# First feed-forward layer of a decoder trunk: six plain pairs instead of seven, operand sums made earlier and in tiles of their own

## The chip, the cores and the metric

The kernel runs on one core of one Trainium2 chip. The metric is the device time of one launch in microseconds (us). Before the change the median of three runs is 2024.97 us (2024.91 to 2026.1).

## The reference

The computation is a decoder trunk of two layers for one sequence of 512 positions and 1024 channels, all in float32. Each layer is a half-weight feed-forward, a mixer (a gated recurrence beside windowed attention) and a second half-weight feed-forward. Only the first feed-forward of layer 0 is touched:

```python
def swiglu(h, w_gate, w_up, w_down):
    return (jax.nn.silu(h @ w_gate) * (h @ w_up)) @ w_down
...
        h = rms_norm(x, gn[0])
        x = x + 0.5 * rms_norm(swiglu(h, w_ffn1_gate[l], w_ffn1_up[l], w_ffn1_down[l]), gn[1])
```

`w_gate` and `w_up` are 1024 x 2816, so there are 22 blocks of 128 hidden channels. For each, a gate product and an up product of 128 x 1024 by 1024 x 512 are needed: one *pair*.

## The kernel before

The activations lie with the channels on the partitions: eight tiles of 128 channels x 512 positions. Every float32 operand is cut into a high part in a reduced format and the low rest, and a product is made of three matrix products, high by high, high by low and low by high (`mm3`, line 412). All products pass through `mm`, so nearly every matmul has line 116.

A pair is made in one of two ways. The *plain* way (`project`, twice) takes 2 x 8 channel tiles x 3 products of 512 columns. The *seven-product* way (`sevenths`) treats the pair as 2 x 2 blocks (gate or up; upper or lower channels; early or late positions) and makes seven block products of 256 columns instead of eight, 7 x 4 x 3 in all. For that it needs sums and differences of the activation tiles: `sums()` makes them for one channel tile k and its partner k+4. Four calls serve all pairs of the layer.

In the first feed-forward of layer 0 the norm is not known when the first products start. So the plain pairs run on x times the gain, and their outputs are scaled afterwards by `rb`, the inverse root mean square spread over the partitions (`gated`, lines 1098 to 1104). `sums()` of the class `First` starts from scaled rows instead: x times gain times `rb` (line 566), then three high/low splits of half tiles (lines 432 and 433: a cast on ScalarE, a subtraction on VectorE), four half-tile sums (lines 490 to 497), and two more splits of 512 columns. That is two scalings, nine further VectorE instructions and five ScalarE casts per call.

Meanwhile x itself is turned to position-major tiles and written to memory (`lay`): eight groups of four 128 x 128 transposes (line 126), each group into one bank of the pool `aux`, copied out by ScalarE and VectorE in turn (line 555) and written by SyncE (line 556). The pool `aux` has three banks; the pool `acc`, for projections, five.

The order of TensorE's instructions is the order in which the code issues them; side jobs such as `lay` are coroutines that are let in when a counter of estimated TensorE time passes their due time (`order.poll`). On the other engines a scheduler orders the instructions by priority. Each engine then works its list strictly in order and waits on counters of the others. Weights come in through SyncE's queue into four buffers, are split by ScalarE (`whi`, line 359) and by VectorE or an adding transfer of GpSimd (`wlo`, lines 363 and 358) into six buffers each.

`FIRST = 7` is the number of plain pairs of this layer; the other 15 are seven-product pairs. `fast(pre, a, FIRST)` makes those.

Of the kernel before, what the change touches and what calls it, by code (L numbers as in the profile page):

```python
# [11 lines left out]
ALU = mybir.AluOpType  # L12
# [21 lines left out]
    head=2600.0, level=5000.0, last=3400.0, chunks=2600.0, states=2600.0, norm=2370.0, gate=8000.0,  # L34
    values=1200.0, scores=2000.0, exp=9000.0, shares=6000.0, turn=1900.0, turned=3000.0, rest=1200.0, lent=4200.0, apart=4000.0, block=2000.0, pair=4000.0, att0=1260.0, att1=12300.0,
)
W32, WS, AHEAD, TAIL, FIRST, EARLY, LATE = 4, 6, 3, 4, 7, 4, 8
TURN = 0
SEVEN = 16
ASIDE = 16  # L40
# [6 lines left out]
def trunk(ctx: ExitStack, tc: tile.TileContext, xin, wall, gains, lbT, hgain, sinks, c_dist, c_mask, c_ident, out):  # L47
    nc = tc.nc
# [11 lines left out]
    def nm(s):  # L60
        seq[0] += 1
        return f"{s}_{seq[0]}"

    def big(dt=F32, shape=None):
        return sb.tile(shape or [P, S], dt, tag="s", name=nm("s"), bufs=SLOTS)
# [10 lines left out]
    def const(shape, name, dt=F32):  # L76
        return cp.tile(shape, dt, tag=name, name=name)
# [35 lines left out]
    order = Order()  # L113
# [16 lines left out]
    g_sb = const([P, DEPTH, 6, KT], "g_sb")  # L130
    nc.scalar.dma_start(g_sb, gains)
    xs = [big() for _ in range(KT)]
# [26 lines left out]
    class Stream:  # L159
# [98 lines left out]
        def quarter(self, it):  # L258
# [16 lines left out]
            if it.kind in ("p1", "p2"):  # L275
                w = raw((u if it.kind == "p1" else v) + q)
            elif it.kind in ("p3", "p5"):
                w = self.b22[q]
            elif it.kind == "p7":

                w = self.b12[q]
                if q == 0:
                    sums(w, w, self.b22[q], ALU.add)
            else:
                w = self.b12[q]
# [5 lines left out]
            if it.kind == "p7" and q + 1 < it.n:  # L291
                sums(self.b12[q + 1], self.b12[q + 1], self.b22[q + 1], ALU.add)
            elif it.kind == "p6":
                sums(self.b22[q], self.b22[q], w, ALU.add)
# [191 lines left out]
    def quarter_sums(a11, a12, a21, a22, flip=False):  # L486


        s, t = big(F32, [P, 2, S // 2]), big(F32, [P, 2, S // 2])
        nc.vector.tensor_tensor(s[:, 0, :], a22, a21, op=ALU.subtract)  # L490
        nc.vector.scalar_tensor_tensor(s[:, 1, :], s[:, 0, :], -1.0, a11, op0=ALU.mult, op1=ALU.subtract)
        if flip:
            nc.vector.tensor_tensor(t[:, 0, :], s[:, 1, :], a12, op=ALU.add)
            nc.vector.tensor_tensor(t[:, 1, :], a21, a11, op=ALU.subtract)
        else:
            nc.vector.scalar_tensor_tensor(t[:, 0, :], s[:, 1, :], -1.0, a12, op0=ALU.mult, op1=ALU.subtract)
            nc.vector.tensor_tensor(t[:, 1, :], a11, a21, op=ALU.subtract)
        return s, t

    def pair_split(v, how=split):  # L500
        return how(v, to=(big(F32R, [P, 2, S // 2]), big(F32R, [P, 2, S // 2])))
# [13 lines left out]
    class First(Quarters):  # L515
# [44 lines left out]
        def sums(self):  # L560

            k = len(self.x56)
            a = []
            for i in range(2):
                f = xs[k + 4 * i]
                nc.vector.scalar_tensor_tensor(f, f, g_sb[:, 0, 0, k + 4 * i : k + 4 * i + 1], self.rb, op0=ALU.mult, op1=ALU.mult)
                a.append([f[:, c] for c in HALF])
            self.x124.append([])
            for v in (a[0][0], a[1][0], a[1][1]):
                x = big(F32R, [P, 2, S // 2])  # L570
                split(v, to=(x[:, 0, :], x[:, 1, :]))
                self.x124[k].append(x)
            for x, v in zip((self.x56, self.x37), quarter_sums(a[0][0], a[1][0], a[0][1], a[1][1])):
                x.append(pair_split(v))
# [420 lines left out]
    def quad(pre, halves):  # L995

        o = [acc() for _ in range(4)]
        blocks = {}
        ws.pinned = halves
        for half in (0, 1) if halves else (None,):  # L1000
            c = WHOLE if half is None else HALF[half]
            for k in range(KT):
                order.until(lambda: pre.have[half or 0] > k)
                for j in range(4):
                    if (k, j) not in blocks:
                        blocks[k, j] = ws.next(uses=2 if halves else 1)
                    if halves and (k, j) == (0, 2):
                        lead(o[j][:, c], blocks[k, j][2], pre.h[k][0][:, c], LEAD_IN[half])
                    wmm(o[j][:, c], blocks[k, j], cut(pre.h[k], c), k == 0, k == KT - 1)
            ws.pinned = False  # L1010
        return o

    def project(pre, get=acc):
        o = get()
        for k in range(KT):
            wmm(o, ws.next(), pre.h[k], k == 0, k == KT - 1)
        return o
# [55 lines left out]
    def fast(pre, a, start):  # L1073
        def early():
            if j == FT - 1:
                for i in range(SEVEN, SEVEN + EARLY):
                    ws.part[i] = split(a[i])

        ws.tight = True
        for j in range(start, FT):  # L1080
            ws.most = AHEAD + (j < FT - 1)
            m = sevenths(pre, early, j == start)
            z = big(F32, [P, 2, H2])
            ws.hold(nc.scalar.activation(out=m[:, 0:2, :], in_=m[:, 0:2, :], func=AF.Silu))

            def gate(m=m, z=z):
                ws.hold(nc.vector.scalar_tensor_tensor(z, m[:, 0:2, :], -1.0, m[:, 2:4, :], op0=ALU.mult, op1=ALU.mult))

            ws.gate = gate
            if j == FT - 1:  # L1090
                ws.product()
            a.append(z.rearrange("p i t -> p (i t)"))
        ws.tight = False

    def ffn(l, n, pre, nxt, halves=True):
        a = []

        def gated(og, ou):
            z, u = big(), big()
            if first:  # L1100
                pin(nc.vector.tensor_tensor(z, og, pre.rb, op=ALU.mult))
                nc.scalar.activation(out=z, in_=z, func=AF.Silu)
                nc.vector.tensor_tensor(u, ou, pre.rb, op=ALU.mult)
                nc.vector.tensor_tensor(u, u, z, op=ALU.mult)
            else:
                nc.scalar.activation(out=z, in_=og, func=AF.Silu)
                pin(nc.vector.tensor_tensor(u, ou, z, op=ALU.mult))
            a.append(u)

        first = isinstance(pre, First)  # L1110
        o = quad(pre, halves)
        if first:
            o.append(project(pre))
            o.append(project(pre, aux))
            order.until(lambda: pre.rb is not None)
        if not first:
            pre.sums()
            pre.sums()
        for j in range(2):
            gated(o[2 * j], o[2 * j + 1])  # L1120
        if first:
            gated(o[4], o[5])
            for j in range(3, FIRST):
                if j > 3:
                    order.until(lambda: pre.laid)
                    pre.sums()
                if j == 4:
                    pre.sums()
                if j == FIRST - 1:
                    ws.most = AHEAD + 2  # L1130
                gated(project(pre), project(pre))
            fast(pre, a, FIRST)
        else:
            pre.sums()
            ws.most = AHEAD + 2
            og = project(pre)
            pre.sums()
            gated(og, project(pre))
            fast(pre, a, 3)
        return down(a, FT, l, n + 1, nxt, True)  # L1140
# [357 lines left out]
    pre = First()  # L1498
# [68 lines left out]
    for l in range(DEPTH):  # L1567
        pre = ffn(l, 0, pre, (l, 2), halves=l > 0)
        pre = mixer(l, pre, (l, 4))
        pre = ffn(l, 4, pre, (l + 1, 0) if l + 1 < DEPTH else None)  # L1570
# [81 lines left out]
```

## Time and profile before

| What | Value |
|---|---|
| Median of three runs | 2024.97 us |
| The profiled execution | 2024.79 us, span 2023.0 us |
| TensorE busy | 2016.2 us, 100% |
| VectorE busy | 1624.3 us, 80% |
| ScalarE busy | 1265.2 us, 63% |
| Granted TensorE clock | 1.0 in all slices |

A busy TensorE means that matmuls follow each other; their ends are modelled, and the next one starts before the last one ends. So the cost of a matmul is read from the distance between starts. The same holds for VectorE and ScalarE, where a row's time reaches a little past the start of the next row. Times at the left of a row are from the start of the span.

### The profile page before, as it was taken

The page shows a single profiled execution, that of the slowest core. Times are in us where ns is not written, and L with a number is a line of the kernel's source. Part 1 is how long each engine was busy: PE and PEld are TensorE (multiplying, and loading weights), DVE is VectorE, ACT ScalarE, POOL GpSimd, SP SyncE. Part 2 cuts the span into 40 slices and gives each one's busy share as a digit, 9 for nine tenths or more (in the row PEclk, how much of TensorE's full clock was granted, in tenths as well). Part 3 has the DMA queues.
Part 4 walks back from the last instruction along what each step waited for, and adds up shares of the span by engine and source line. Part 5 has one row for each costly group of instructions (what it writes and reads, how often), then busy time and mean ns, then how long its engine had stood idle before and what let it go on. Part 6 is the DMA issues. An engine that isn't in the chain of part 4 may idle for free.

```text
span 2023.0 us, 36425 instructions
## 1 busy us (share of the span) xinstructions
PE 2016.2 (100%) x13553; PEld 1809.1 (89%) x13553; DVE 1624.3 (80%) x2894; ACT 1265.2 (63%) x2213; POOL 268.3 (13%) x318
## 2 busy tenths in 40 slices
PE   9999999999999999999999999999999999999998
PEld 8899988877898999998899998898778989999987
DVE  5888899767786788888998888977686858888888
ACT  7566687447364566658766666864554646666684
POOL 0111140000000011113211111400000100111140
PEclk9999999999999999999999999999999999999999
DMA  8688798311246368879768888872122554788794
GB/s 257 159 193 198 177 203 244 109 63 64 83 104 208 112 158 190 193 189 208 202 170 196 196 190 203 189 223 86 61 74 63 151 182 123 170 193 200 175 202 122
DMA packets 166801, 328.07 MB, mean 162 GB/s; under 512 B 19072, under 2 KB 85088, under 8 KB 166624
## 3 DMA queue, kind: packets, MB, share of 16 engines
q1 hardware_dynamic: 122416, 228.16, 34.1%
q0 software_dynamic: 44064, 97.54, 28.5%
q8 instruction: 106, 1.74, 0.3%
q14 instruction: 71, 0.58, 0.1%
q10 hardware_dynamic: 144, 0.05, 0.0%
HBM read 213.43 MB, written 14.73 MB: 113 GB/s over the span
## 4 chain that ended last, share of the span: by engine, by line
PE 93%; DVE 3%; ACT 1%; DMA 1%; issue 1%; SPq 0%; DVEq 0%; ACTq 0%
PE acc L116 71%; PE aux L116 20%; PE aux L126 2%; DVE wlo L296 1%; DVE s L264 1%; DMA w<-wall 1%; PE acc L126 0%; ACT whi L288 0%; DVE s L968 0%; SPq L244 0%; ACT s L442 0%; ACT s L443 0%; DVE wlo L363 0%; DVE s L863 0%; DVE s L433 0%
## 5 line engine op out<-in xcount | busy, mean ns | idle before, releaser
L116 PE MATMUL acc<-s,whi 128*128 128x256 f32 (+1 forms) x4998 | 1018.9, 303 | 0.0
L116 PEld LDWEIGHTS acc<-s,whi 128*128 128x128 f32 x4998 | 791.5, 188 | 46.6 <-issue 3.2
L116 PE MATMUL acc<-s,wlo 128*128 128x256 f32 (+1 forms) x2488 | 752.5, 302 | 0.1
L116 PEld LDWEIGHTS acc<-s,wlo 128*128 128x128 f32 x2488 | 467.9, 188 | 23.3 <-DVE wlo L363 0.4
L116 PE MATMUL acc<-whi,s 128*128 128x512 f32 x1360 | 441.5, 393 | 0.0
L359 ACT CAST whi<-w 128x1024 fp32r<-128x1024 f32 (+1 forms) x310 | 286.1, 926 | 195.0 <-PE acc L116 124.5
L358 POOL DMA_DIRECT2D wlo<-w x178 | 154.6, 869 | 1200.2 <-ACT wlo L355 715.0
L116 PEld LDWEIGHTS acc<-whi,s 128*128 128x128 f32 x1360 | 255.3, 188 | 57.1 <-issue 3.2
L116 PE MATMUL acc<-wlo,s 128*128 128x512 f32 x680 | 265.5, 390 | 0.2 <-DVE wlo L296 0.2
L355 ACT ACTIVATE wlo<-w 128x1024 fp32r<-128x1024 f32 (+1 forms) x178 | 154.6, 869 | 137.1 <-PE aux L116 98.2
L116 PE MATMUL aux<-s,whi 128*128 128x256 f32 (+1 forms) x1296 | 226.9, 278 | 0.0
L359 ACT CAST whi<-tt 128x1024 fp32r<-128x1024 f32 x160 | 168.4, 1053 | 83.2 <-DVE tt L341 43.0
L363 DVE TENSOR_TENSOR wlo<-w,whi 128x1024 fp32r<-128x1024 f32 (+1 forms) x132 | 157.4, 1205 | 78.3 <-ACT whi L359 78.1
L363 DVE TENSOR_TENSOR wlo<-tt,whi 128x1024 fp32r<-128x1024 f32 x160 | 195.4, 1221 | 9.9 <-ACT whi L359 7.3
L116 PEld LDWEIGHTS aux<-s,whi 128*128 128x128 f32 x1296 | 195.8, 188 | 1.1 <-issue 0.5
L116 PE MATMUL aux<-s,wlo 128*128 128x256 f32 (+1 forms) x648 | 179.8, 277 | 0.0
L116 PEld LDWEIGHTS acc<-wlo,s 128*128 128x128 f32 x680 | 127.8, 188 | 27.0 <-DVE wlo L296 2.1
L116 PE MATMUL aux<-whi,s 128*128 128x512 f32 x432 | 143.7, 390 | 0.0
L444 POOL DMA_DIRECT2D s<-s x128 | 111.1, 967 | 223.5 <-ACT s L432 104.7
L116 PEld LDWEIGHTS aux<-s,wlo 128*128 128x128 f32 x648 | 121.6, 188 | 0.4
L296 DVE TENSOR_TENSOR wlo<-s,whi 128x512 fp32r<-128x512 f32 x160 | 102.7, 686 | 9.9 <-ACT whi L288 9.9
L1070 DVE TENSOR_TENSOR m<-aux,s 128x512 f32<-128x512 f32 x80 | 55.2, 690 | 52.0 <-PE aux L116 51.5
(184 smaller groups left out, 2485.1 us busy)
## 6 DMA issues: line engine op xcount, KB each, us to landing
w<-wall SPq DMA_DIRECT2D x267, 512.0 KB, 3.9
wlo<-w POOLq DMA_DIRECT2D x98, 512.0 KB, 5.4
w<-wall SPq DMA_DIRECT2D x224, 128.0 KB, 3.5
wlo<-w POOLq DMA_DIRECT2D x80, 256.0 KB, 4.2
s<-wall SPq DMA_DIRECT2D x128, 128.0 KB, 4.2
s<-s POOLq DMA_DIRECT2D x64, 256.0 KB, 4.6
x_d<-s SPq DMA_DIRECT2D x48, 256.0 KB, 4.7
s<-x_d SPq DMA_DIRECT2D x48, 256.0 KB, 5.1
```

The costliest lines, as they stand in the source:

```text
L116: nc.tensor.matmul(o, lhsT, rhs, start=start, stop=stop)
L126: nc.tensor.transpose(o, src, ident)
L264: pin(nc.vector.tensor_tensor(o[c], x[c], y[c], op=op))
L296: pin(nc.vector.tensor_tensor(it.lo[:, h[c]], w[c], it.hi[:, h[c]].bitcast(F32), op=ALU.subtract))
L355: i = nc.scalar.mul(it.lo[:, c], w[:, c], -1.0)
L358: nc.gpsimd.dma_start(it.lo[:, c].bitcast(F32), w[:, c], accum_op=ALU.add)
L359: i = nc.scalar.copy(it.hi[:, c], w[:, c])
L363: self.hold(nc.vector.tensor_tensor(it.lo[:, c], w[:, c], it.hi[:, c].bitcast(F32), op=ALU.subtract))
L444: nc.gpsimd.dma_start(lo.bitcast(F32), src, accum_op=ALU.add)
L1070: ws.hold(nc.vector.tensor_tensor(m[:, 1:3, :], pairs[2], v[:, ::-1, :], op=ALU.add))
```

## The change

`FIRST` goes from 7 to 6. The scaled rows of `sums()` are written to new tiles, no longer over x; so `sums()` needs not wait until `lay` has read x, and the condition on `pre.laid` is gone. The four calls now stand ahead of the fourth, fifth and sixth plain pair (one, one and two); before, two stood ahead of the fifth and one each ahead of the sixth and seventh.

```diff
-W32, WS, AHEAD, TAIL, FIRST, EARLY, LATE = 4, 6, 3, 4, 7, 4, 8
+W32, WS, AHEAD, TAIL, FIRST, EARLY, LATE = 4, 6, 3, 4, 6, 4, 8
...
             for i in range(2):
-                f = xs[k + 4 * i]
-                nc.vector.scalar_tensor_tensor(f, f, g_sb[:, 0, 0, k + 4 * i : k + 4 * i + 1], self.rb, op0=ALU.mult, op1=ALU.mult)
+                f = big()
+                nc.vector.scalar_tensor_tensor(f, xs[k + 4 * i], g_sb[:, 0, 0, k + 4 * i : k + 4 * i + 1], self.rb, op0=ALU.mult, op1=ALU.mult)
                 a.append([f[:, c] for c in HALF])
...
             for j in range(3, FIRST):
-                if j > 3:
-                    order.until(lambda: pre.laid)
+                pre.sums()
+                if j == FIRST - 1:
                     pre.sums()
-                if j == 4:
-                    pre.sums()
-                if j == FIRST - 1:
                     ws.most = AHEAD + 2
                 gated(project(pre), project(pre))
             fast(pre, a, FIRST)
```

The change moves instructions on ScalarE and VectorE. In the rows below a name is a tile with its running number, and the brackets name the counters waited for. First TensorE in the fourth plain pair, at the fourth group of transposes, which goes to `aux_520` before and to `aux_547` in the change. Before:

```order
L116 MATMUL acc_513<-s_132,whi_338 128x512 [waits DVE_49]
L116 MATMUL acc_513<-s_133,whi_338 128x512
L116 MATMUL acc_513<-s_132,wlo_339 128x512
L116 MATMUL acc_513<-s_144,whi_338 128x512
L116 MATMUL acc_513<-s_145,whi_338 128x512
L116 MATMUL acc_513<-s_144,wlo_339 128x512
L126 MATMUL aux_520<-ident,s_74 128x128 [waits DVE_49]
```

In the change:

```order
L116 MATMUL acc_540<-s_132,whi_338 128x512
L116 MATMUL acc_540<-s_133,whi_338 128x512
L116 MATMUL acc_540<-s_132,wlo_339 128x512
L116 MATMUL acc_540<-s_144,whi_338 128x512
L116 MATMUL acc_540<-s_145,whi_338 128x512
L116 MATMUL acc_540<-s_144,wlo_339 128x512
L126 MATMUL aux_547<-ident,s_74 128x128 [waits PE_49,Activation_49]
```

The place on TensorE is the same; the counter waited for is now ScalarE's. The value waited for is that of the copy that empties the bank of the first group of transposes, `s_502<-aux_497`. Before, it was VectorE's line 1103, which empties the bank of the third pair's up projection.

Next ScalarE, from the second pair's SiLU (`s_445`) and the third's (`s_451`) to the copies of line 555. Before:

```order
L1102 ACTIVATE s_445<-s_445 128x512 [waits DVE_49]
L555 COPY s_475<-aux_470 128x512 [waits PE_49]
L1102 ACTIVATE s_451<-s_451 128x512 [waits DVE_49]
L359 CAST whi_671<-w_72_384 128x1024 [waits DMAHW7_49,PE_49,Activation_49]
L555 COPY s_510<-aux_505 128x512 [waits PE_49]
L355 ACTIVATE wlo_672<-w_72_384 128x1024
L555 COPY s_539<-aux_534 128x512 [waits PE_49]
```

In the change:

```order
L1102 ACTIVATE s_445<-s_445 128x512 [waits DVE_49]
L1102 ACTIVATE s_451<-s_451 128x512 [waits DVE_49]
L432 CAST s_461<-s_457 128x256 [waits DVE_49]
L359 CAST whi_675<-w_72_384 128x1024 [waits DMAHW7_49,PE_49,Activation_49]
L432 CAST s_464<-s_459 128x256 [waits DVE_49]
L432 CAST s_467<-s_459 128x256
L355 ACTIVATE wlo_676<-w_72_384 128x1024 [waits PE_49]
L432 CAST s_476<-s_470 128x512 [waits DVE_49]
L432 CAST s_480<-s_471 128x512 [waits DVE_49]
L555 COPY s_502<-aux_497 128x512
L555 COPY s_537<-aux_532 128x512 [waits PE_49]
```

The copy of the first group (`s_475<-aux_470` before, `s_502<-aux_497` now) stood one place behind a SiLU; it now stands behind five casts of the first `sums()` and two instructions of a weight split.

Last VectorE, at the end of the fourth `sums()`, in the change. Ahead of it stand all the other three calls, the fourth and fifth pair's scaling of outputs and the weight sums of the first two seven-product pairs:

```order
L566 SCALAR_TENSOR_TENSOR s_748<-s_73,g_sb,s_395 128x512 [waits DMAHW1_49]
L566 SCALAR_TENSOR_TENSOR s_750<-s_77,g_sb,s_395 128x512
L433 TENSOR_TENSOR s_752<-s_748,s_752 128x256 [waits Activation_49]
L345 TENSOR_TENSOR tt_848<-tt_845,w_104_530 128x512
L363 TENSOR_TENSOR wlo_844<-tt_845,whi_843 128x1024 [waits DMASW3_49,PE_49,Activation_49]
L433 TENSOR_TENSOR s_755<-s_750,s_755 128x256 [waits Activation_49]
L433 TENSOR_TENSOR s_758<-s_750,s_758 128x256 [waits Activation_49]
L490 TENSOR_TENSOR s_761<-s_750,s_748 128x256
L497 TENSOR_TENSOR s_762<-s_748 128x256
L491 SCALAR_TENSOR_TENSOR s_761<-s_761,s_748 128x256 [waits DVE_49]
L496 SCALAR_TENSOR_TENSOR s_762<-s_761,s_750 128x256 [waits DVE_49]
L433 TENSOR_TENSOR s_768<-s_761,s_767 128x512 [waits DMAHW3_49,Activation_49]
```

Before, the scalings of this call stood far ahead, among the first two calls, and the weight sums of the second seven-product pair began only behind line 496. From the second seven-product pair on, the lists of all engines are the same in both kernels but for the tiles' numbers, and so is everything behind the layer. On SyncE the eight writes of line 556 now stand together, behind the weight loads of the first two seven-product pairs; before, two loads stood among them. The row of `rows_d` stands ahead of the eighth write now, and behind it before.

## The prediction

> **What bounds the kernel now.** I read the page's first part and its chain first, then the busy times by stage, then the engines' instructions in order of time between 40 and 108 us. From the page:
>
> ```profile
> PE 2016.2 (100%) x13553; PEld 1809.1 (89%) x13553; DVE 1624.3 (80%) x2894; ACT 1265.2 (63%) x2213; POOL 268.3 (13%) x318
> ...
> PE 93%; DVE 3%; ACT 1%; DMA 1%; issue 1%; SPq 0%; DVEq 0%; ACTq 0%
> ```
>
> TensorE hardly pauses, and 93% of the chain that ended last is its own work. So a matmul removed is time won, and any pause that appears on TensorE is time lost: nothing behind it has slack to take it up. The busy times by stage around the change:
>
> ```profile
> core 0: us, PE busy (x) PEld busy (x) DVE busy (x) ACT busy (x) POOL busy (x), PEclk, DMA share, GB/s
> ...
> 40.00:60.00 20.00, 20.00 (x106) 16.68 (x105) 11.52 (x20) 11.47 (x18) 2.58 (x3) 1.00 0.93 235
> 60.00:80.00 20.00, 20.00 (x90) 16.58 (x89) 19.66 (x40) 10.65 (x19) 0.86 (x1) 1.00 0.56 142
> 80.00:100.00 20.00, 20.00 (x142) 18.56 (x141) 16.42 (x28) 11.53 (x18) 3.44 (x4) 1.00 0.53 128
> 100.00:120.00 20.00, 20.00 (x178) 20.00 (x178) 16.70 (x25) 13.16 (x17) 3.44 (x4) 1.00 0.85 195
> ```
>
> TensorE never waits in these stages. VectorE is full between 60 and 80 us, where the four `sums()` run, and has 8.5 us free in the twenty before. The change moves `sums()` into that free stretch, and takes one plain pair's time away from them.
>
> **The plain pair: -1.36 us.** TensorE's rows of a plain pair, of the start of the seven-product pairs, and the chain through two of the latter:
>
> ```profile
> 82.83 0.62 PE L116 MATMUL acc<-s,whi 128*128 128x512 f32 x2
> ...
> 88.27 0.51 PE L116 MATMUL acc<-s,whi 128*128 128x144 f32 x3
> ...
> 98.07 6.80 PE acc L116 x60
> 104.87 2.72 PE aux L116 x24
> 107.59 6.80 PE acc L116 x60
> ```
>
> From 82.83 to 88.27 lie the last eight channel tiles, 24 products of 512 columns: 5.44 us, 0.2267 each. A plain pair has 48: 10.88. A seven-product pair repeats after 107.59 - 98.07 = 9.52 us (84 products of 256 columns). The difference is 1.36. The lead product of 144 columns is made once in both kernels. The number of `sums()` is the same, and one more seven-product combination on VectorE and ScalarE lies beside TensorE work there, as in the other 15 pairs.
>
> **The fourth group of transposes: +2.5 us.** `aux` has three banks. The fourth group needs the bank of the first; the copy that frees it now stands on ScalarE behind five casts of the first `sums()` and a weight split, and two of the casts wait for VectorE. The rows for this, TensorE, ScalarE and VectorE one after the other:
>
> ```profile
> 49.12 0.60 PE L126 MATMUL aux<-ident,s 128*128 128x128 f32 x4
> 52.80 0.60 PE L126 MATMUL aux<-ident,s 128*128 128x128 f32 x4
> ...
> 44.28 0.59 ACT L555 COPY s<-aux 128x512 f32<-128x512 f32 x1 [0.64 <-PE aux L126]
> ...
> 47.31 1.05 ACT L359 CAST whi<-w 128x1024 fp32r<-128x1024 f32 x1 [1.67 <-PE acc L116]
> 48.27 0.58 ACT L555 COPY s<-aux 128x512 f32<-128x512 f32 x1
> 48.74 1.06 ACT L355 ACTIVATE wlo<-w 128x1024 fp32r<-128x1024 f32 x1
> ...
> 56.08 1.06 ACT L355 ACTIVATE wlo<-w 128x1024 fp32r<-128x1024 f32 x1
> 57.04 0.62 ACT L1102 ACTIVATE s<-s 128x512 f32<-128x512 f32 x1
> ...
> 62.04 0.62 ACT L432 CAST s<-s 128x512 fp32r<-128x512 f32 x1
> 62.56 1.05 ACT L355 ACTIVATE wlo<-w 128x1024 fp32r<-128x1024 f32 x1
> ...
> 80.61 0.70 ACT L432 CAST s<-s 128x256 fp32r<-128x256 f32 x2
> ...
> 44.89 0.68 DVE L1103 TENSOR_TENSOR s<-aux,s 128x512 f32<-128x512 f32 x1
> ...
> 59.67 0.42 DVE L490 TENSOR_TENSOR s<-s,s 128x256 f32<-128x256 f32 x1
> 60.01 0.42 DVE L497 TENSOR_TENSOR s<-s 128x256 f32<-128x256 f32 x1
> ```
>
> The first copy ran at 44.28, long before 49.12. In the change ScalarE goes on thus. The cast of `whi` starts at 47.31 as before, since it waits for the first plain projection of this pair to let go of its buffer. Start to start, a 1024-column instruction takes 0.96 (56.08 to 57.04, 47.31 to 48.27), a cast of 512 takes 0.52 (62.04 to 62.56), a cast of 256 takes 0.30 (two in 0.70, the last 0.40). So the casts of `s_464` and `s_467` start at 48.27 and 48.57, the `wlo` at 48.87, the cast of `s_476` at 49.83. The cast of `s_480` waits for VectorE: `s_464` is there at 48.68, then two subtractions, line 491 and line 497 at 0.34 each (59.67 to 60.01), and line 496 with its full 0.42, which ends at 50.46. With 0.04 for each handing over, the cast starts at 50.5, the copy at 51.0, and ends 0.59 later at 51.6. TensorE stands at the transposes from 49.12 to 51.65: 2.5 us, with all its later work behind it. From below, ScalarE's list alone without VectorE's wait gives 47.31 + 0.96 + 0.60 + 0.96 + 0.52 + 0.52 + 0.59 = 51.46, so 2.3; from above, each of the six instructions ahead of the copy with its full time, 0.1 more, gives 3.1. The later copies follow at once and empty the other banks: group five comes 1.8 us behind, no further wait.
>
> **The operands of the first seven-product pair: +1.5 us.** VectorE's copy of the sixth group follows its transposes, so 2.5 us later than in this row:
>
> ```profile
> 53.44 0.69 DVE L555 COPY s<-aux 128x512 f32<-128x512 f32 x1 [2.98 <-PE aux L126]
> ...
> 63.60 0.75 DVE L566 SCALAR_TENSOR_TENSOR s<-s,g_sb,s 128x512 f32<-128x512 f32 x1
> 64.27 1.70 DVE L433 TENSOR_TENSOR s<-s,s 128x512 fp32r<-128x512 f32 x4
> ...
> 74.38 1.29 DVE L433 TENSOR_TENSOR s<-s,s 128x512 fp32r<-128x512 f32 x2 [0.27 <-ACT s L432]
> ...
> 76.19 0.69 DVE L341 TENSOR_TENSOR tt<-w 128x512 f32<-128x512 f32 x1
> 76.79 0.69 DVE L343 TENSOR_TENSOR tt<-tt,w 128x512 f32<-128x512 f32 x1
> ...
> 78.12 1.22 DVE L363 TENSOR_TENSOR wlo<-tt,whi 128x1024 fp32r<-128x1024 f32 x1
> 79.26 0.68 DVE L1101 TENSOR_TENSOR s<-acc,s 128x512 f32<-128x512 f32 x1
> ...
> 85.14 0.69 DVE L433 TENSOR_TENSOR s<-s,s 128x512 fp32r<-128x512 f32 x1
> ```
>
> At about 56.55 the fourth pair's line 1101 starts. From there to `s_768`, the split of the fourth call's differences, VectorE's list has 19 instructions of 512 columns at 0.60 (76.19 to 76.79), six scalings at 0.66 (63.60 to 64.27), 21 of 256 at 0.335 and three of 1024 at 1.14 (78.12 to 79.26): 11.4 + 4.0 + 7.0 + 3.4 = 25.8. I add 2.3 of waits, an estimate put together from the same rows: 0.4 for the fourth pair's SiLU, which stands behind a late copy; 0.4 for the end of the fifth pair's up projection; 0.6 for a cast of the third call behind a weight split on ScalarE; 0.4 for the last cast of the chain; 0.5 in small steps. So `s_768` is there at 56.55 + 25.8 + 2.3 + 0.69 = 85.3. TensorE begins the seven-product pairs at 88.27 - 10.88 + 2.5 = 79.9 and wants `s_768` as the fourth channel tile of the third product, after 34 products of 0.1133 and the lead: 83.8. It waits 1.5. As a cross-check: before, the same split ended at 85.8 and was wanted at 92.2, 6.4 to spare; the wish moves up 8.4, the split 0.5. From below, without the waits, it comes at 83.0 and nothing is lost: 0. From above, with twice the waits, 3.8. I take 1.5. The next operand, 0.6 later, is wanted 1.4 later.
>
> **Costed at nothing.** The weights: transfers of the third seven-product pair stand on SyncE behind the eight writes of line 556. Counted along VectorE's list from 56.55, the last copy ahead of them falls at about 64, and the first weight sums, which free their buffers, end at about 67; they are wanted at about 92. GpSimd's adding transfers start in the same relation to their products. The tiles for scaled rows free themselves within the call. If that cover were gone, each late weight would stop TensorE directly.
>
> **The sum**: -1.36 + 2.5 + 1.5 = +2.6 us. The profiled execution took 2024.79 us (span 2023.0 and 1.8 around it), 0.2 below the median of the runs: 2027.4 against the one, 2027.6 against the other. I say 2027.5, 0.13% above before.
>
> **Rivals.** About 0.2%, or 4 us, is what a measurement of this kernel can tell from no change.
>
> *No pause appears* (10%). ScalarE's copy comes in time and VectorE keeps up, so the pair's 1.36 us are won: 2024.97 - 1.36 = 2023.6. For it: VectorE's 8.5 free us between 40 and 60. Against it: the list on ScalarE has no way past the `wlo` and the casts, and the 49.12 - 47.31 = 1.8 us hold only three of the six instructions ahead of the copy.
>
> *TensorE falls back to its starting speed after the pause* (8%), slower than before. The start of the kernel and a product of the same kind later:
>
> ```profile
> 1.07 4.96 PE L116 MATMUL aux<-ones 128*128 128x128 f32 x24 [1.07 <-DVE eps_t L139]
> ...
> 35.94 1.02 PE L116 MATMUL aux<-s,ones 128*128 128x512 f32 x2
> 36.39 1.02 PE L116 MATMUL aux<-s,whi 128*128 128x512 f32 x2
> 37.25 0.40 PE L116 MATMUL aux<-s,wlo 128*128 128x512 f32 x1
> ```
>
> Twelve float32 products of 128 columns (two records each) took 4.96 us, 0.41 each. The one of 512 at 35.94, with two of 0.2267 behind it, took 1.31 to 37.25, so 0.86, or 0.21 per 128. Starting cold cost 4.96 - 12 x 0.21 = 2.4 us. Were that paid again behind a pause of 2.5: +2.6 + 2.4 = +5.0, 2029.9. It decides from the pause's length; the granted clock stands at 1.00 in every stage above, and none holds such a pause, so the trace can't exclude it.
>
> The Trainium skill (page "TensorE: Matmul & The Clock Gate", Part 1, the HAM clock gate) says that the clock is halved only after an idle window of about 3.4 us. By that rule 2.5 us cost nothing more and the sum stays; were the rule met, an estimate from it is half of 3.4 us, 1.7, and 2029.2. The trace agrees as far as the start goes, which ran at half speed.
>
> *VectorE's backlog is worse* (8%), also slower. If its waits from 56.6 to 84.6 come to 4.6 us, not 2.3, the second pause is 3.8: +4.9, 2029.8. It decides from about 3.7 us of waits. For it: VectorE has no gap there to catch up in. Against it: before, the one wait that shows over the four calls is the 0.27 at 74.38.
>
> **How the numbers follow.** The forecast holds 72%, with its own range 2026.2 to 2028.7 (pauses of 2.3 to 3.1 and 0.4 to 2.0). 2% are left for what I don't see. The range 2024.2 to 2029.9 leaves out the first rival and what goes beyond the others. Faster by over 0.2% would be below 2020.9: 3%, what I don't see and the far edge of the first rival. Slower by over 0.2%, above 2029.0: the second and third rival, 16%, and 2% of the forecast's edge: 18%. Within 0.2%: 79%.
>
> **What would show it.** In the profile of the changed kernel: on TensorE a pause of some 2.5 us at the fourth group of line 126, near 49 us, ended by ScalarE's line 555, and that copy at 51 us, not 44; a second pause of about 1.5 us in small pieces between 82 and 86 us, ended by lines 432 and 433; the seven-product pairs still 9.52 us apart, and shifted by 2.6 us from the second on; all later stages as long as before; the granted clock 1.00 throughout. The prediction is wrong if TensorE has no pause at 49 us, if the pair was worth other than 1.36, or if pauses appear behind the first seven-product pair.

## The result and the profile after

| | Before | After |
|---|---|---|
| Median, measured side by side | 2025.28 us (9 runs, 2024.71 to 2026.15) | 2030.28 us (9 runs, 2028.95 to 2036.35) |
| Ratio | | 1.0032, 95% interval 1.0021 to 1.0043 |
| Profiled execution, span | 2024.79, 2023.0 us | 2029.45, 2027.7 us |
| Line 1070 (the sum that ends a pair) of the first seven-product pair that both have, from the span's start | 98.11 us | 101.32 us |
| From the last such row of this feed-forward to the span's end | 1789.3 us | 1790.8 us |

The kernel became slower, by 5.0 us, and 0.4 beyond the upper end of the predicted range. The spread says as much as the median: three of the nine runs lie at 2034.85 to 2036.35, the other six at 2028.95 to 2031.28. The nine of before lie within 1.5 us.

The waits of TensorE between 40 and 120 us in the changed kernel (total, how often, longest); there were none before:

```profile
PE aux L126 <- ACT s L555: 2.4, 1, 2.4
PE acc L116 <- ACT s L432: 0.5, 1, 0.5
PE acc L116 <- DVE s L433: 0.3, 1, 0.3
```

These are the two pauses that the prediction placed, with the lines that it named. The rows around them, ScalarE first, then TensorE (start, time, in brackets the idle time and what ended it):

```profile
47.53 1.05 ACT L359 CAST whi<-w 128x1024 fp32r<-128x1024 f32 x1 [0.63 <-PE acc L116]
48.49 0.70 ACT L432 CAST s<-s 128x256 fp32r<-128x256 f32 x2
49.10 1.06 ACT L355 ACTIVATE wlo<-w 128x1024 fp32r<-128x1024 f32 x1
50.06 1.28 ACT L432 CAST s<-s 128x512 fp32r<-128x512 f32 x2
51.25 1.07 ACT L555 COPY s<-aux 128x512 f32<-128x512 f32 x2
...
51.88 0.66 PE L126 MATMUL aux<-ident,s 128*128 128x128 f32 x4 [2.37 <-ACT s L555]
...
80.27 0.51 PE L116 MATMUL acc<-s,whi 128*128 128x144 f32 x3
...
82.77 0.66 PE L116 MATMUL acc<-s,whi 128*128 128x256 f32 x2
...
85.08 0.38 PE L116 MATMUL acc<-s,whi 128*128 128x256 f32 x1 [0.51 <-ACT s L432]
85.81 0.39 PE L116 MATMUL acc<-s,whi 128*128 128x256 f32 x1 [0.34 <-DVE s L433]
```

The copy starts at 51.25 behind casts and a weight split; before it ran at 44.28. The stages of the changed kernel, as they were shown of before:

```profile
40.00:60.00 20.00, 17.63 (x94) 14.41 (x93) 14.49 (x27) 11.12 (x19) 1.72 (x2) 1.00 0.93 259
60.00:80.00 20.00, 20.00 (x90) 16.48 (x89) 19.06 (x36) 10.13 (x18) 1.72 (x2) 1.00 0.31 72
80.00:100.00 20.00, 19.15 (x162) 18.48 (x162) 18.24 (x29) 12.15 (x20) 2.59 (x3) 1.00 0.61 156
100.00:120.00 20.00, 20.00 (x179) 20.00 (x178) 16.18 (x24) 13.27 (x18) 3.45 (x4) 1.00 0.77 181
```

TensorE's busy time now falls short by 2.4 us in the first stretch and by 0.85 in the third. The granted clock (the 1.00 ahead of the DMA share) shows no fall in this execution. The first common pair, before and after:

```profile
98.11 0.69 DVE L1070 TENSOR_TENSOR m<-aux,s 128x512 f32<-128x512 f32 x1 [0.84 <-PE aux L116]
```

```profile
101.32 0.69 DVE L1070 TENSOR_TENSOR m<-aux,s 128x512 f32<-128x512 f32 x1 [0.84 <-PE aux L116]
```

So at the first common pair the profiled execution is 3.2 us late, and at the end 4.7 (2027.7 - 2023.0). The prediction said 2.6 and nothing more. The long executions, at 10 us above before, are not in this trace at all. The experiments ask what they are.

### The profile page after: what moved, and what is told of

It is laid out like the page before. It is cut to its first block, busy times and chain, and to the rows that moved or that the text cites. A ratio compares the mean times of both kernels' runs of the same rounds, so it can differ in the third digit from the quotient of the medians.

```text
span 2027.7 us, 36505 instructions
## 1 busy us (share of the span) xinstructions
PE 2017.4 (99%) x13589; PEld 1809.9 (89%) x13589; DVE 1630.7 (80%) x2902; ACT 1268.2 (63%) x2216; POOL 268.9 (13%) x318
## 4 chain that ended last, share of the span: by engine, by line
PE 91%; DVE 5%; ACT 2%; issue 1%; DMA 1%; SPq 0%; DVEq 0%; ACTq 0%
PE acc L116 69%; PE aux L116 20%; PE aux L126 2%; DVE wlo L296 1%; DVE s L264 1%; DMA w<-wall 1%; DVE s L968 1%; PE acc L126 0%; DVE wlo L363 0%; DVE s L433 0%; ACT whi L288 0%; ACT s L442 0%; SPq L244 0%; ACT s L443 0%; DVE s L863 0%
```

## The experiments

The theories, by letter. **A**: the two pauses less the plain pair, 2.6 to 3.2 us, are all. **B**: behind a pause TensorE's clock falls, in some executions. **C**: the ends of the down stages take longer. **D**: one more pause, somewhere else. **E**: in some executions one stage runs with slower products.

### The changed kernel again, and each pause alone

`e1` is the changed kernel. In `e2` the fourth pair's gate projection is issued ahead of `sums()`, so that ScalarE has the copies of line 555 ahead of the casts. A line with a plus is added, one with a minus taken out:

```diff
+                og = project(pre) if j == 3 else None
                 pre.sums()
...
-                gated(project(pre), project(pre))
+                gated(og or project(pre), project(pre))
```

`e3` is `e2` with the calls spread one, two, one, so that VectorE has the last operands in time:

```diff
+                if j == 4:
+                    pre.sums()
                 if j == FIRST - 1:
-                    pre.sums()
```

`e4` is the changed kernel with seven plain pairs (`FIRST = 7`), with the calls where they are in the change: one, one and two ahead of the fourth, fifth and sixth pair.

> The changed kernel once more. Theory A (the two pauses on TensorE add to the time and nothing else happens): before + 3.2 us, the shift that its first profile shows behind the first seven-product pair, 2028.5, and runs as close together as those of before, within 1.5 us. Theory B (behind the pause of 2.4 us at the fourth group of transposes the TensorE clock falls back in some executions): the fastest runs at 2029, others up to 2036, and the longer ones with a mean granted clock of 0.998 to 0.999. Theory C (the shift alone makes the ends of the down projections slower): 2029 to 2030 with close runs and clock 1.000, and the extra in four steps at the ends of the down stages.

> The first operand sums stand between the gate and the up projection of the fourth pair, so that ScalarE copies the first groups of transposes ahead of them. It takes away the pause of 2.4 us at 49 us; the second one (1.5 us in three pieces of 0.2 to 0.7) stays. Theory A: -1.4 + 1.5 = +0.1 against before. Theory B: the same +0.1, and the wide spread is gone, since no piece is longer than 0.8 us. Theory C: +1 to +1.5, from the ends of the down stages.

> As the one before, and the third and fourth operand sums stand ahead of the fifth pair instead of the sixth (one, two and one call): by the lists and the durations of the rows neither pause is left. Theories A and B: the plain pair's 1.36 us are won, 2023.9 against 2025.3, runs within 1.5 us. Theory C: -0.5 to +0.5.

> Seven plain pairs as before, but with scaled rows in their own places and the sums ahead of the fourth, fifth and sixth pair (one, one, two calls). The pause at 49 us is there (2.4 us), the second is not, and nothing is won. Theory A: +2.4, 2027.7, close runs. Theory B: fastest runs at 2027.7, others up to 7 us longer with a mean clock below 1. Theory C: +3 to +4, close runs.

| | Pauses in the profile | Median (range) us | Ratio (95%) | Span |
|---|---|---|---|---|
| before, same chip | none | 2024.62 (2023.79 to 2026.15) | | |
| e1 | 2.4 and 0.5 + 0.3 | 2031.01 (2028.24 to 2036.68) | 1.0034 (1.0024 to 1.0045) | 2027.3 |
| e2 | 0.5 + 0.3 | 2026.04 (2025.25 to 2032.49) | 1.0013 (1.0004 to 1.0022) | 2023.5 |
| e3 | none | 2024.73 (2023.61 to 2025.74) | 0.9999 (0.999 to 1.0008) | 2022.3 |
| e4 | 2.4 | 2027.63 (2026.77 to 2030.93) | 1.0017 (1.0008 to 1.0026) | 2025.1 |

What follows: both pauses come from the order of the casts, copies and sums, and without them the loss is gone. But the plain pair's 1.36 us are not won: A and B had `e3` at 2023.9. In the medians `e2`, `e3` and `e4` lie 1.4, 0.1 and 3.0 us above before, at or within the bounds that C gave. C does not explain the spread, though, since it had close runs, and neither does A; B had none in `e2`. Three of the eleven executions of `e2` lie at 2031.2 to 2032.5, some 6 us above its other eight; `e1` has three at 2033.7 to 2036.7. `e3` and `e4` have none of these. In `e4` there is another step: six executions at 2026.8 to 2027.6, five at 2028.8 to 2030.9. So each pause seems to bring a loss of its own, and not in every execution: 2 us behind the first, 6 behind the second.

### Single executions of the changed kernel, and one long pause

Three profiles of the changed kernel, each of another execution, and `e6`: `e2` with two calls between the fourth pair's projections and one each ahead of the fifth and sixth, so that ScalarE's copies come late again, but VectorE's last operands in time.

```diff
                 og = project(pre) if j == 3 else None
                 pre.sums()
+                if j == 3:
+                    pre.sums()
                 if j == FIRST - 1:
-                    pre.sums()
```

> The changed kernel, one more profile. Some executions of it took 5 to 8 us more than the fastest, and none of the profiles shows one. The mean granted clock of the long ones (0.998 to 1.000) does not tell them from the fast ones, which speaks against theory B. Theory B would still show a stretch with a granted clock below 1 behind 49 us. Theory D: in the long executions something behind the pauses (a weight's transfer, a split) comes late and TensorE pauses once more, by 2 to 8 us, somewhere in the seven-product pairs or in the down projection; the profile of a long execution would name the place. If this execution is a fast one (2028 to 2029.5), it shows only the two pauses again.

> The same as the look before: a fast execution (2028 to 2029.5) with only the two pauses, or a long one (2031 to 2037), whose profile tells theory B (clock below 1) from theory D (one more pause on TensorE at a certain place).

> The same as the look before: a fast execution (2028 to 2029.5) with only the two pauses, or a long one (2031 to 2037), whose profile tells theory B (clock below 1) from theory D (one more pause on TensorE at a certain place).

> Six plain pairs; two operand sums between the fourth pair's projections, one ahead of the fifth and one ahead of the sixth. By the lists there is one pause of 4.5 us on TensorE at the seventh group of transposes, near 55 us, ended by ScalarE's copies, and no second one. Theory A: -1.4 + 4.5 = +3.1 against before and close runs. Theory B: a pause of 4.5 us, longer than 2.4, makes the clock fall in most executions, so +5 to +6 with a granted clock below 1 behind it. Theory D: +3.1 in the fastest, and a spread of several us as with the shorter pause.

The three took 2030.94, 2027.91 and 2029.09 us; before on the same chip 2024.6. In the first the clock fell. TensorE's part of the chain of waits behind the first pause (start, time, how many), in this execution:

```profile
52.08 0.66 PE aux L126 x4
52.74 2.17 PE acc L116 x6
54.91 0.85 PE aux L126 x4
55.77 1.78 PE acc L116 x6
57.54 0.44 PE aux L126 x4
```

and the same in the profile of the changed kernel that was shown first:

```profile
51.88 0.66 PE aux L126 x4
52.54 1.38 PE acc L116 x6
53.92 0.44 PE aux L126 x4
54.36 1.39 PE acc L116 x6
55.75 0.44 PE aux L126 x4
```

From the transposes behind the pause to the ones two groups later it is 57.54 - 52.08 = 5.46 us against 55.75 - 51.88 = 3.87: 1.6 us lost. The stretches of the long one, with the granted clock ahead of the DMA share:

```profile
50.00:54.00 4.00, 1.92 (x9) 1.64 (x10) 3.46 (x7) 2.46 (x5) 0.86 (x1) 0.88 0.87 227
54.00:58.00 4.00, 4.00 (x18) 3.28 (x17) 0.00 (x0) 0.59 (x1) 0.00 (x0) 0.69 1.02 330
58.00:62.00 4.00, 4.00 (x23) 3.28 (x23) 3.63 (x6) 1.41 (x3) 0.00 (x0) 1.00 0.49 185
```

Four transposes take 0.85 us there instead of 0.44, so TensorE ran at half speed. Half speed for a time of t lowers the mean of a stretch of 4 us by t / 8: (0.12 + 0.31) x 8 = 3.4 us at half speed. This is B, the prediction's second rival, in one execution and not in the next, with the same pause of 2.4 us in both. Of the seven profiles in this study with this pause it shows in two.

`e6` took 2030.07 us (2029.58 to 2032.77), ratio 1.0029 (1.0018 to 1.004), with one pause and a clock that fell behind it:

```profile
59.21 0.66 PE L126 MATMUL aux<-ident,s 128*128 128x128 f32 x4 [4.28 <-ACT s L555]
...
58.00:62.00 4.00, 2.79 (x10) 2.29 (x11) 3.99 (x8) 2.32 (x5) 0.00 (x0) 0.73 0.47 173
```

It has no pause inside the seven-product pair. Its executions lie between 2029.6 and 2030.8 but for one at 2032.77, so the long ones seem to belong to the second pause. C is not the cause of the spread: in all 20 profiles here the time from this stage's last common pair to the span's end lies between 1788.6 and 1790.8 us. Open are that one execution of `e6` and three of `e4`, at 2029.57 to 2030.93: those three lie 2.4 to 3.8 us above the middle of the fast six of `e4`, more than one fall of the clock cost. None of the four has a profile.

### What the long executions are

Four single executions of `e2`, which has the second pause alone, until a long one had a profile.

> The kernel with the second pause alone, one more profile. Three of its eleven executions took 6 us more than the others, two of them with a mean granted clock of 1.000, so the clock is not their cause. Theory D: in such an execution TensorE pauses once more, for 5 to 7 us, at one place behind the second pause, and the row behind it names what was late. Theory E: no pause, but a stage in which products follow each other more slowly, by 5 to 7 us in all. A fast execution (2025 to 2026.5) shows only the second pause.

> The same as the look before: a long execution (2031 to 2033) would show one more pause of 5 to 7 us (theory D) or a slower stage (theory E); a fast one (2025 to 2026.5) only the second pause.

> The same as the look before: a long execution (2031 to 2033) would show one more pause of 5 to 7 us (theory D) or a slower stage (theory E); a fast one (2025 to 2026.5) only the second pause.

> The same as the look before: a long execution (2031 to 2033) would show one more pause of 5 to 7 us (theory D) or a slower stage (theory E); a fast one (2025 to 2026.5) only the second pause.

They took 2025.27, 2026.25, 2025.71 and 2032.06 us. The largest group of TensorE's products between 90 and 140 us (count, busy time, mean ns of one, idle time), in the first:

```profile
L116 PE MATMUL acc<-s,whi 128*128 128x256 f32 x216 | 37.0, 276 | 0.0
```

and in the fourth:

```profile
L116 PE MATMUL acc<-s,whi 128*128 128x256 f32 x205 | 36.5, 281 | 0.0
```

No idle time in either, and fewer products in the same 50 us. The whole stretch, first and fourth:

```profile
90.00:140.00 50.00, 50.00 (x444) 50.00 (x443) 41.74 (x60) 32.42 (x44) 8.88 (x11) 1.00 0.83 192
```

```profile
90.00:140.00 50.00, 50.00 (x427) 50.00 (x426) 39.88 (x57) 31.04 (x42) 8.95 (x11) 1.00 0.79 185
```

444 products against 427, with the clock at 1.00 and the weight loads (the second busy time) without a gap in both. The chain says it most sharply; 60 products and 24 products, first:

```profile
89.36 6.80 PE acc L116 x60
96.17 2.72 PE aux L116 x24
```

fourth:

```profile
89.49 7.07 PE acc L116 x60
96.55 2.83 PE aux L116 x24
```

A product takes 0.1178 us instead of 0.1133, a pair 9.89 instead of 9.52, and it stays so up to the stage's last pair: 140.35 us instead of 135.56 from its first common pair to its last. With the pair before them that is 5.2 us. The seven-product stage of the next feed-forward has its 173.15 us in both. This is E: a second, slower rhythm in which products follow each other.

### What decides the rhythm

Each seven-product stage begins with one `lead` product of 144 columns (line 1049). Theory **F**: it sets the fast rhythm, and the second pause, which lies behind it, lets the rhythm fall at random. **G**: it has no part in it. `f1` is `e2` and `f3` the changed kernel, each with a second lead product ahead of the second seven-product pair of this layer; `f2` is the kernel before without the lead product in this layer:

```diff
 f1, f3
-            m = sevenths(pre, early, j == start)
+            m = sevenths(pre, early, j in (start, start + 1 if start == FIRST else start))
 f2
-            m = sevenths(pre, early, j == start)
+            m = sevenths(pre, early, j == start and start != FIRST)
```

> The kernel with ScalarE's copies first, which keeps the second pause (0.9 us, inside the first seven-product pair), and a second lead product of 144 columns ahead of the second seven-product pair, behind that pause. It adds work (0.06 us) and takes none away. Theory F (the lead product sets the rhythm in which TensorE's products follow their weight loads; the second pause breaks it, and behind it the rhythm is at random, now and then the slow one, until a new lead product): the executions at 2031 to 2032.5 vanish, all lie within 2025.0 to 2026.8, and the pairs of the profile are 9.52 us apart. Theory G (the rhythm is decided by something else, and the lead product has no part in it): three or four of eleven executions at 2031 to 2032.5 as before, the others at 2025.3 to 2026.4.

> The kernel before, with the lead product left out in the first feed-forward alone; the other three feed-forwards keep theirs. It takes away 0.06 us of work and makes no pause. Theory F: the rhythm is at random from the start of the seven-product pairs, so some of the executions (a third, or all of them) have pairs 9.89 us apart instead of 9.52, which is 5.5 us over 15 pairs: 2030 to 2031, the others 2024.6. Theory G: no change, 2024.6 in all executions, pairs 9.52 apart.

> The changed kernel, with both pauses, and the second lead product ahead of the second seven-product pair. Theory F: no execution above 2032: 2027.5 to 2029.5 with the granted clock full, 1.6 more in those where the clock falls behind the first pause. Theory G: about a third of the executions at 2033 to 2037, as in the changed kernel, and a median near 2030.

| | Median (range) us | Ratio to before (95%) |
|---|---|---|
| before, same chip | 2024.61 (2023.6 to 2025.67) | |
| f1 | 2030.87 (2026.18 to 2032.33) | 1.0026 (1.0015 to 1.0037) |
| f2 | 2030.0 (2029.54 to 2030.88) | 1.0027 (1.0017 to 1.0038) |
| f3 | 2033.6 (2033.19 to 2035.71) | 1.0047 (1.0035 to 1.006) |

`f2` came out as F said, in all eight executions: without the lead product, and without any pause, the stage runs in the slow rhythm from its start, and the median is 5.4 us longer. (One execution has a profile; the others are placed by their time.) So G fell. The chain of `f2`:

```profile
95.86 2.83 PE aux L116 x24
98.68 7.07 PE acc L116 x60
105.75 2.83 PE aux L116 x24
```

But F fell with `f1` and `f3`. The second lead product did not mend the rhythm: five of the seven executions of `f1` were long, and all five of `f3`. The chains show why. `f1`, an execution of 2026.18 us; the 61 products are the second pair's first sixty and the new lead:

```profile
86.74 2.83 PE aux L116 x24
89.57 6.93 PE acc L116 x61
96.50 2.72 PE aux L116 x24
```

`f3`, one of 2035.71 us:

```profile
90.57 2.72 PE aux L116 x24
93.29 7.18 PE acc L116 x61
100.47 2.83 PE aux L116 x24
```

In `f1` the rhythm was slow ahead of the new lead product and fast behind it; in `f3` it was the other way round. So theory **H**: a lead product switches from the one rhythm into the other. Its rival **H'**: it draws the rhythm by chance. `f4` and `f5` are the kernel before with two and with three lead products, one after the other, in place of the one; `f6` is `e3` once more:

```diff
-        if first:
+        for _ in range(first):
             lead(p1, w.hi[:, :P], pre.operand(1)[0][0], LEAD)
...
-            m = sevenths(pre, early, j == start)
+            m = sevenths(pre, early, (j == start) * (2 if start == FIRST else 1))
```

> The kernel before, with two lead products of 144 columns one after the other at the start of the first seven-product stage, where it has one. Adds 0.06 us of work. Theory H (each lead product puts TensorE from the one rhythm into the other; the plain products hand over in the slow one): two of them lead back to the slow rhythm, pairs 9.89 us apart in all executions, 2030. Theory H' (a lead product sets the rhythm by chance, mostly to the slow one where the products ahead of it are of 256 columns): slow in some executions and not in others. Theory F in its first form (a lead product sets the fast rhythm): 2024.7, pairs 9.52 apart.

> The kernel before, with three lead products in place of one. Adds 0.12 us of work. Theory H: fast rhythm again, 2024.7 in all executions, pairs 9.52 us apart. Theory H': some executions at 2030.

> The kernel without pauses once more (ScalarE's copies first, sums in calls of one, two and one), to see whether the plain pair's 1.36 us arrive at the end: its first common product came 1.23 us earlier than before and its span was 0.7 shorter, but the median of eleven runs was the same. If they arrive: 1.0 to 1.4 below the kernel before on the same chip. If the later stages give them back: the same within 0.5. No execution at 2030 or above in either case, since TensorE has no pause ahead of the seven-product pairs.

| Kernel before with | Executions | Median (range) us | Pairs apart |
|---|---|---|---|
| no lead product (f2) | 8 | 2030.0 (2029.54 to 2030.88) | 9.89 |
| one (before, all runs here) | 90 | 89 within 2023.6 to 2026.2, one at 2029.36 | 9.52 |
| two (f4) | 8 | 2030.85 (2029.64 to 2031.81) | 9.89 |
| three (f5) | 10 | 2025.17 (2024.5 to 2026.27) | 9.52 |

The stretch of 50 us of `f4`, and of `f5`:

```profile
90.00:140.00 50.00, 50.00 (x427) 50.00 (x426) 38.79 (x55) 30.17 (x40) 8.61 (x10) 1.00 0.74 177
```

```profile
90.00:140.00 50.00, 50.00 (x444) 50.00 (x443) 40.51 (x58) 31.52 (x42) 8.60 (x10) 1.00 0.77 182
```

H holds: slow, fast, slow, fast with none, one, two and three lead products, without an exception in the 26 executions of `f2`, `f4` and `f5`. Each has one execution with a profile, the others are placed by their time. Of the 90 of before, the one at 2029.36 lies where the slow ones do; it has no profile, and what it held is open. In the three later feed-forwards, which keep one lead product each, the seven-product stage takes the same time within 0.03 us in all 20 profiles. A lead product costs about 0.12 us itself (6.93 against 6.80 for the sixty without it, above), not the 0.06 of the expectations. Whether it must have 144 columns, or whether any one product more would do, was not tried.

H also fits the second pause. Behind it, counted by their time, 6 of 20 executions of the changed kernel and 4 of 15 of `e2` were slow. In `f1` and `f3`, where the next lead product turns the rhythm round, the long executions became the rule: 10 of 12. No long execution of the changed kernel itself has a profile; that it holds the slow rhythm is taken from the fourth of `e2`, from `f3`, which has both pauses too, and from the times.

`f6` had a median of 2025.04 us (2024.18 to 2025.91) against 2024.75, ratio 1.0 (0.9991 to 1.0009). Its first common pair came at 97.06, 1.05 earlier than before, but no gain arrived at the end, as in `e3`.

## Why the prediction failed, step by step

*The plain pair: -1.36 us.* Right in its place: without pauses the first common pair came 1.23 (`e3`, 96.88 against 98.11) and 1.05 us (`f6`) earlier. It does not arrive at the end of either kernel (below).

*The fourth group of transposes: +2.5.* Right. The transposes went from 49.12 to 51.88; 0.2 of that was there already at 41 us, at the start of this pair's first projection, so 2.5. ScalarE's list ran as worked out: `whi` at 47.53, two casts and the `wlo` each 0.2 behind the forecast, the wait for VectorE's line 496, the copy at 51.25.

*The operands of the first seven-product pair: +1.5.* Right in place and nearly in size. From the lead product to the first product into `aux` behind it, the time was 6.92 us before (88.27 to 95.19). In the changed kernel it was 88.88 - 80.27 = 8.61: 1.7 lost, in three steps at 82.8, 85.1 and 85.8.

Here are the rows for this, first before, then after:

```profile
95.19 0.39 PE L116 MATMUL aux<-s,whi 128*128 128x256 f32 x2
```

```profile
88.88 0.39 PE L116 MATMUL aux<-s,whi 128*128 128x256 f32 x2
```

-1.36 + 2.5 + 1.7 + 0.2 from ahead of 41 us is 3.0 of the 3.2 measured. Had this been all, as *The sum* took it, the time would have been about 2028.

**The step that failed is what the prediction held constant behind the pauses**, its list under *What would show it*: "the seven-product pairs still 9.52 us apart", "all later stages as long as before", "the granted clock 1.00 throughout". Each of the three was wrong, the first two in some of the executions:

- *9.52 us apart.* Not in 6 of 20 executions. No step and no rival had this. I took a pause as time that is lost once; in some executions the second one also moved the products of a whole stage into another rhythm, 5.2 us. The prediction had the lead product before its eyes (in the row at 88.27) and costed it as the same in both kernels. What it does lies in what follows it, and the pause comes between.
- *The granted clock.* The rival "TensorE falls back to its starting speed after the pause" had been given 8%, as something that happens or does not. It happens in some executions: two of seven profiles with this pause. Its price was 1.6 us, where the start rows had given 2.4.
- *Later stages as long as before.* From the stage's last common pair to the span's end the profile of after took 1.5 us longer. Over all profiles, 15 with six plain pairs took 1789.0 to 1790.8 us, mean 1789.9; five with seven took 1788.6 to 1789.4, mean 1789.0. So about 0.9 us is lost there, which takes up most of the plain pair's gain. In the profile of after it comes in steps of 0.1 to 0.5 us, mostly towards the ends of the down stages; the largest, at 1327 us, holds a wait of 0.3 us for VectorE's line 296. These instructions stand in the same order in both kernels. The number of pairs is not all: the five profiles of the changed kernel and that of `f3` have a mean of 1790.3, the six of `e2` and `f1` one of 1789.6. Why time is lost there, no run here settles.

The times follow: 2025.0 + 3.2 + 0.9 = 2029.1 for an execution with neither fall nor slow rhythm; 1.6 more with the clock's fall, which makes 2030.7; 5 more with the slow rhythm, 2034 and above. The runs lie near these three places, and their median, 2030.28, between the first two. Of the 2.8 us from 2027.5 to the median, 0.6 was there at the first common pair and about 0.9 came in the later stages; the rest is the median's place among the groups. All runs but the profiled one are placed by their time alone.

The Trainium skill (page "TensorE: Matmul & The Clock Gate", Part 1, the HAM clock gate) has the clock halved after an idle window of about 3.4 us, and speaks of a free-running window. The trace agrees with the length, 3.4 us at half speed, and a free-running window fits a fall that comes in one execution and not in the next. It differs on the threshold: a pause of 2.4 us was enough. By this rule the prediction let 2.5 us cost nothing more; its price for a fall, 1.7, was close to the 1.6 measured.

*No pause appears*: refuted by the waits. *VectorE's backlog is worse*: no; the split was ready 0.5 us later than said, not 2.3.

Open are three things: what the two rhythms are inside TensorE; what decides the rhythm behind a pause; and the 0.9 us in the later stages. No kernel of these beats the one before by more than the measurement tells.

## What to carry to other kernels

Where TensorE never waits, a pause is not only its own length: ask what state the unbroken stream carried over it, the clock and the rhythm of the products, and price the second for the rest of the stage. Where weight loads fill a stage without a gap, compare the distance of a few dozen products between profiles before trusting a sum. When the runs of one kernel fall into groups, profile single executions until one of each group is caught; the median's own trace may hold none of the cause.

## What the runs showed of the hardware

- Products of 256 columns whose weight loads leave no gap have two rhythms, 0.1133 and 0.1178 us each, at a granted clock of 1.00. In an unbroken stream a rhythm lasted to the last pair of its stage (140.35 against 135.56 us). One product of 144 columns more switched to the other: slow, fast, slow, fast with none, one, two and three. Behind waits of 0.5 and 0.3 us in the stream the rhythm differed from execution to execution: slow in 10 of 35 by their time.
- A TensorE pause of 2.4 us brought 3.4 us at half clock in two of seven profiles, a pause of 4.3 us in the one profile with it. Each fall behind the pause of 2.4 us that was measured against an execution without it cost 1.6 us.
